# Seven block products for eight in the second MLP matrix of a transformer block, with sums of the squares on GpSimd

## The chip, the cores and the metric

The kernel runs on one core of a Trainium2 chip. The metric is the device time of one execution in microseconds (us); lower is better. All matrices are 32-bit floats; matmuls run in the replicated form `float32r`, and every factor is split into a high and a low part (H and L), so that one product of two 128-row tiles is three matmuls: H by H, H by L, L by H.

## The reference

One layer of a diffusion block on a latent stream of 1024 tokens by 1024 channels: a mixer (attention and a state-space branch), then a squared-ReLU MLP. The change touches only the MLP and what is done with its result:

```python
def sq_relu_mlp(h, w1, b1, w2, b2):
    return jnp.square(jax.nn.relu(h @ w1 + b1)) @ w2 + b2

h2_l = modulate(rms_norm(x, norm2_g[l]), sh2_l, sc2_l)
x = x + g2_l * sq_relu_mlp(h2_l, w_mlp1[l], b_mlp1[l], w_mlp2[l], b_mlp2[l])
```

Here `h` is 1024 x 1024, `w1` is 1024 x 4096, `w2` is 4096 x 1024. The squares between the two matrices are called s below, transposed: 4096 rows (hidden units) by 1024 columns (tokens).

## The kernel before

The MLP is the last part of the kernel. All loads and stores are issued from SyncE's one queue, in order. Each engine takes its own instructions in order; for the MLP that order comes out of a planner that places each instruction at the time at which its cost model finds it ready, except for the first 14 loads of the first matrix, where TensorE's order is that of the text.

**First matrix (`first`, `mlp1`).** It already takes seven products of 2 x 2 blocks for eight (the Winograd form of Strassen). The hidden units are taken in 16 pairs of 128-row tiles; the tokens are two halves of 512. For each pair two 512 KB weight tiles r1 and r2 come into `wr` (three buffers). VectorE forms sums of them (`cs`, one buffer; `c4`, one buffer; in place in r2), and `wsplit` makes the H part on ScalarE and the L part on GpSimd (`wH`, `wL`, four buffers). The products B11 and B21 of 14 pairs are made ahead by `first`; the loop over `mlp1(p)` then makes T2, T1, T3, B22 and T4, each 12 matmuls into one PSUM bank (`mm`, six buffers). VectorE adds the products up (`u2`, `u4`, `u3`), and `c_out` adds the bias, ScalarE applies ReLU and square, and the 128 x 512 block of squares is stored to a DRAM tensor `s_d`.

**Second matrix.** No blocks are saved. The 32 tiles of s (128 hidden units by 1024 tokens) and of w2 (128 by 1024) are loaded, split (both L parts on GpSimd), and taken in batches of one, one, thirteen times two, and four tiles. For each batch all 8 x 2 blocks of the output are multiplied into PSUM (three matmuls a tile) and added by VectorE to an accumulator `acc` in SBUF. In the last batch VectorE also multiplies by the gate row `g2row` and adds the residual, and the rows are stored. `mod2` is a small vector product that makes the gate row; ten steps of it run among the batches.

The pools of the first matrix (`h2a`, `n2`, `ml`, `h2b`) are left before the pool `mq` of the second is opened over the same space. The first two tiles of the second matrix are prepared ahead in the pool `wp`, which lives on.

Of the kernel before, what the change touches and what calls it, by code (L numbers as in the profile page):

```python
# [48 lines left out]
def block_kernel(ctx, tc, io, out, dbg=None):  # L49
    nc = tc.nc  # L50
    V, S, G, T = nc.vector, nc.scalar, nc.gpsimd, nc.tensor
    LD = nc.sync
# [47 lines left out]
    wp = ctx.enter_context(pool("wp"))  # L100
    dr = ctx.enter_context(pool("dr", space=DRAM))
# [17 lines left out]
    def wload(src, shape):  # L119
        raw = wp.tile([128, 1024], F32, name="wr", tag="wr", bufs=3)  # L120
        LD.dma_start(raw[:, :int(np.prod(shape))].rearrange("p (a b) -> p a b", a=shape[0]), src)
        return raw

    def wtile(src, shape, scale_row=None, low=None, raw=None):

        n = int(np.prod(shape))
        if raw is None:
            raw = wload(src, shape)
        H = wp.tile([128, 1024], F32R, name="wH", tag="wH", bufs=4)
        L = wp.tile([128, 1024], F32R, name="wL", tag="wL", bufs=4)  # L130
        if scale_row is not None:
            sr = scale_row if shape[0] == 1 else scale_row[:, None, :].to_broadcast([128, shape[0], shape[1]])
            rr = raw[:, :n] if shape[0] == 1 else raw[:, :n].rearrange("p (a b) -> p a b", a=shape[0])
            V.tensor_tensor(rr, rr, sr, op=OP.mult)
        S.activation(H[:, :n], raw[:, :n], AF.Copy)  # L135
        (low or G).tensor_tensor(L[:, :n], raw[:, :n], H[:, :n], op=OP.subtract)  # L136
        return H, L

    def mm3(ps, pairs):

        n = len(pairs)
        for i, (lH, lL, rH, rL) in enumerate(pairs):
# [229 lines left out]
    ws_u, acc = [], []  # L372
# [32 lines left out]
    todo = [(q, kk) for q in range(1, 4) for kk in range(4)]  # L405
# [12 lines left out]
    for q in range(4):  # L418
# [5 lines left out]
        if q == 0:  # L424
# [6 lines left out]
            p = trb()  # L431
            for i in range(3):
# [12 lines left out]
                            op=OP.mult)  # L445
# [173 lines left out]
    for nm in ("re", "im"):  # L619
        p = trb()  # L620
# [122 lines left out]
    for g8 in range(0, NG, 16):  # L743
        p = trb()
# [608 lines left out]
    def mmc():  # L1353
        return psC.tile([128, 512], F32, name="mm", tag="mm", bufs=6)
# [271 lines left out]
    NP = 16  # L1626
    NA = 14
    t1_d = dr.tile([NA, 128, 512], F32, name="t1_d")
    s_d = dr.tile([32, 128, 1024], F32, name="s_d")

    def w1_raw(ft):
        return wload(w1[:, ft * 128:(ft + 1) * 128].rearrange("(a p) n -> p a n", p=128), (8, 128))
# [13 lines left out]
    def r_tile():
        return ml.tile([128, 512], F32, name="r", tag="r", bufs=3)

    def act_out(r, ft, f):
        S.activation(r, r, AF.Square)  # L1650
        LD.dma_start(s_d[ft][:, f * 512:(f + 1) * 512], r)

    def b1(ft):
        return cols[:, R_B1 + ft:R_B1 + ft + 1]

    def c_out(ps, add, ft, f):
        r = r_tile()
# [23 lines left out]
    def mlp1(p):  # L1681
        r1, r2 = w1_raw(2 * p), w1_raw(2 * p + 1)
        cs = ml.tile([128, 1024], F32, name="cs", tag="cs", bufs=1)
        c4 = ml.tile([128, 512], F32, name="c4", tag="c4", bufs=1)
        a, b = slice(0, 512), slice(512, 1024)
        if p >= NA:
            t1 = first(p, wsplit(r1))
        else:
            t1 = t1_tile()
            LD.dma_start(t1, t1_d[p])  # L1690
        V.tensor_tensor(cs[:, a], r2[:, a], r2[:, b], op=OP.add)
        V.tensor_tensor(cs[:, b], cs[:, a], r1[:, a], op=OP.subtract)
        wc = wsplit(cs)
        V.tensor_tensor(c4, r1[:, b], cs[:, b], op=OP.subtract)
        V.tensor_tensor(r2[:, a], r1[:, a], r2[:, a], op=OP.subtract)
        wr = wsplit(r2)
        w4 = wsplit(c4, 512)
        u2, u3, u4 = (ml.tile([128, 512], F32, name=nm, tag=nm, bufs=1) for nm in ("u2", "u3", "u4"))
        V.tensor_tensor(u2, prod(wc, 1, "T2"), t1, op=OP.add)
        V.tensor_tensor(u4, prod(wc, 0, "T1"), u2, op=OP.add)  # L1700
        p7 = prod(wr, 0, "T3")
        V.tensor_tensor(u3, p7, u2, op=OP.add)
        c_out(p7, u4, 2 * p + 1, 1)
        c_out(prod(w4, 0, "B22"), u4, 2 * p, 1)
        c_out(prod(wr, 1, "T4"), u3, 2 * p + 1, 0)

    man_ = tc.manual_schedule(engines={mybir.EngineType.PE})
    man_.__enter__()
# [9 lines left out]
    def w2_src(ft):
        return w2[ft * 128:(ft + 1) * 128, :].rearrange("p (a n) -> p a n", a=1)

    def s_src(ft):
        return s_d[ft].rearrange("p (a n) -> p a n", a=1)

    pre = [(wtile(s_src(0), (1, 1024)), wtile(w2_src(0), (1, 1024)))]
    ml_.__exit__(None, None, None)
    n2_.__exit__(None, None, None)
    h2a_.__exit__(None, None, None)
    h2b_.__exit__(None, None, None)
    mq = ctx.enter_context(pool("mq", reuse_waits="tile"))
    acc2 = [mq.tile([128, 1024], F32, name=f"acc{t}") for t in range(8)]  # L1730
    bb2 = mq.tile([128, 1024], F32, name="bb2")
    LD.dma_start(bb2, bcast_rows(io["b_mlp2"], 1024))

    def mq_split(raw, nm, bufs):
        H = mq.tile([128, 1024], F32R, name=nm + "H", tag=nm + "H", bufs=bufs)
        L = mq.tile([128, 1024], F32R, name=nm + "L", tag=nm + "L", bufs=bufs)
        S.activation(H, raw, AF.Copy)  # L1737
        G.tensor_tensor(L, raw, H, op=OP.subtract)  # L1738
        return H, L

    def mlp2_tiles(ft):
        rs = wload(s_src(ft), (1, 1024))
        rw_ = mq.tile([128, 1024], F32, name="rw2", tag="rw2", bufs=3)
        LD.dma_start(rw_.rearrange("p (a b) -> p a b", a=1), w2_src(ft))
        return mq_split(rs, "s", 6), mq_split(rw_, "w", 6)

    BL = [[0], [1]] + [[b, b + 1] for b in range(2, 28, 2)] + [[28, 29, 30, 31]]
    NBL = len(BL)
    pre2 = [(mq_split(wload(s_src(1), (1, 1024)), "f", 2), mq_split(wload(w2_src(1), (1, 1024)), "f", 2))]
    m2_todo = list(range(30, 40))  # L1750
    m2a = mq.tile([128, 1024], F32, name="m2a")
    m2r = mq.tile([128, 512], F32, name="m2r")
    for bi, fts in enumerate(BL):
        last_ = bi == NBL - 1
        tiles = (pre, pre2)[bi] if bi < 2 else [mlp2_tiles(ft) for ft in fts]
        for t in range(8):
            if last_:
                xr = mq.tile([128, 1024], F32, name="rw2", tag="rw2", bufs=3)
                LD.dma_start(xr, x2_d[t])
            tk = slice(t * 128, (t + 1) * 128)  # L1760
            for n in range(2):
                o = slice(n * 512, (n + 1) * 512)
                ps = mmc()
                mm3(ps, [(s_[0][:, tk], s_[1][:, tk], w_[0][:, o], w_[1][:, o]) for s_, w_ in tiles])
                a_ = acc2[t][:, o]
                V.tensor_tensor(a_, a_ if bi else bb2[:, o], ps, op=OP.add)  # L1766
                if last_:
                    V.tensor_tensor(a_, a_, g2row[:, o], op=OP.mult)
                    V.tensor_tensor(a_, a_, xr[:, o], op=OP.add)
                    if t == 7:  # L1770
                        LD.dma_start(out_v[t][:, o], a_)
            if last_ and t < 7:
                LD.dma_start(out_v[t], acc2[t])
        if 3 <= bi < 8:
            for _ in range(2):
                mod2(m2_todo.pop(0), m2a, m2r, trc)
            if bi == 7:
# [28 lines left out]
```

## Time and profile before

| | |
|---|---|
| median of 3 runs | 1910.69 us (1907.51 to 1912.46) |
| profiled execution: its time | 1909.88 us |
| profiled execution: its span | 1908.2 us |
| TensorE busy in the span | 1841.1 us (96%) |
| VectorE, ScalarE, GpSimd busy | 1279.1, 691.9, 895.4 us |

The span runs from the first to the last instruction that the profiler saw; the time of the execution is 1.7 us longer. A share of busy time is a mean over stages with different limits, so the stages of the MLP have to be looked at one at a time. PE is TensorE, PEld its weight loads, DVE VectorE, ACT ScalarE, POOL GpSimd, SP SyncE. A matmul's listed duration overlaps with the next one's; what it costs is the distance from one start to the next.

### The profile page before, as it was taken

How to read it: one execution, taken by the hardware profiler on the slowest of the kernel's cores; microseconds unless marked ns; L12 is line 12 of the kernel's file. 1: busy time of each engine (PE TensorE's matmuls, PEld its weight loads, DVE VectorE, ACT ScalarE, POOL GpSimd, SP SyncE). 2: the span in 40 equal slices, each digit the busy share in tenths (PEclk: the TensorE clock that was granted, in tenths of full speed). 3: DMA queues.
4: the chain of work that ended last, by engine and by line, in shares of the span. 5: the costliest groups of instructions: out<-in, count | busy, mean ns of one | idle time of the engine just before them, and what ended most of it. 6: DMA issues, size and time to landing. Idle time of an engine off the chain costs nothing. (4 is left out here: it accounts for less than half of the span.)

```text
span 1908.2 us, 25109 instructions
## 1 busy us (share of the span) xinstructions
PE 1841.1 (96%) x9250; PEld 1402.6 (74%) x9250; DVE 1279.1 (67%) x2194; ACT 691.9 (36%) x1016; POOL 895.4 (47%) x471
## 2 busy tenths in 40 slices
PE   7889999998999999999989999999999999999998
PEld 4668888887776556556547777887888877878887
DVE  5989998738897787777645455486454457545556
ACT  4542222244314555555442121455444541111110
POOL 2232333313425777777784453375444564443330
PEclk9989999999999999999999999999999999999999
DMA  9412222221222000000006664355554465333213
GB/s 308 97 56 71 76 77 78 76 85 46 84 71 78 18 23 23 23 23 18 22 13 207 213 209 144 116 177 182 155 155 152 126 218 178 110 107 104 89 55 144
DMA packets 179339, 200.72 MB, mean 105 GB/s; under 512 B 28112, under 2 KB 128260, under 8 KB 179216
## 3 DMA queue, kind: packets, MB, share of 16 engines
q1 hardware_dynamic: 179216, 199.11, 32.6%
q8 instruction: 73, 1.20, 0.3%
q14 instruction: 50, 0.41, 0.1%
HBM read 154.85 MB, written 44.09 MB: 104 GB/s over the span
## 5 line engine op out<-in xcount | busy, mean ns | idle before, releaser
L1202 POOL TENSOR_TENSOR accP<-accP,P 128x1024 f32<-128x1024 f32 x96 | 240.9, 2510 | 20.9 <-ACT P L1184 15.7
L1766 DVE TENSOR_TENSOR acc<-acc,mm 128x512 f32<-128x512 f32 x240 | 162.5, 686 | 127.6 <-PE mm L145 127.6
L136 POOL TENSOR_TENSOR wL<-wr,wH 128x1024 fp32r<-128x1024 f32 (+1 forms) x58 | 135.9, 2351 | 197.9 <-ACT wH L135 187.0
L1184 ACT ACTIVATE P<-sT 128x1024 f32<-128x1024 f32 x160 | 163.8, 1026 | 116.6 <-PE sT L1180 114.1
L1088 DVE TENSOR_REDUCE m<-mx 128x1 f32<-128x512 f32 x240 | 154.5, 686 | 76.1 <-PE mx L1086 69.7
L143 PE MATMUL mm<-wH,sH 128*128 128x512 f32 x480 | 187.3, 390 | 1.3 <-DVE acc L1766 1.2
L144 PE MATMUL mm<-wL,sH 128*128 128x512 f32 x480 | 186.8, 389 | 0.0
L145 PE MATMUL mm<-wH,sL 128*128 128x512 f32 x480 | 186.7, 389 | 0.0
L1197 PE MATMUL pv<-P,Vt 128*64 128x512 f32 x640 | 150.5, 600 | 0.0
L1738 POOL TENSOR_TENSOR sL<-wr,sH 128x1024 fp32r<-128x1024 f32 x30 | 72.2, 2406 | 152.0 <-ACT sH L1737 152.0
L135 ACT ACTIVATE wH<-wr 128x1024 fp32r<-128x1024 f32 (+1 forms) x62 | 61.9, 1005 | 216.2 <-PE mm L144 96.4
L1737 ACT ACTIVATE sH<-wr 128x1024 fp32r<-128x1024 f32 x30 | 31.6, 1054 | 226.5 <-issue 160.7
L1177 PE MATMUL sT<-Q,KH 128*128 128x512 f32 x320 | 105.3, 410 | 2.2 <-ACT P L1184 2.2
L143 PEld LDWEIGHTS mm<-wH,sH 128*128 128x128 f32 x480 | 90.1, 188 | 22.5 <-DVE acc L1766 2.9
L145 PEld LDWEIGHTS mm<-wH,sL 128*128 128x128 f32 x480 | 90.1, 188 | 18.9
L144 PEld LDWEIGHTS mm<-wL,sH 128*128 128x128 f32 x480 | 90.1, 188 | 18.2
L143 PE MATMUL mm<-hH,wH 128*128 128x512 f32 x248 | 101.1, 408 | 0.0
L1180 PE MATMUL sT<-Q,K 65*128 65x512 f32 x320 | 100.9, 396 | 0.0
L145 PE MATMUL mm<-hH,wL 128*128 128x512 f32 x248 | 97.7, 394 | 0.0
L144 PE MATMUL mm<-hL,wH 128*128 128x512 f32 x248 | 97.3, 392 | 0.0
L1197 PEld LDWEIGHTS pv<-P,Vt 128*64 128x64 f32 x640 | 41.7, 136 | 71.6 <-issue 62.3
L1666 POOL TENSOR_TENSOR wL<-wr,wH 128x1024 fp32r<-128x1024 f32 x32 | 76.8, 2405 | 36.6 <-ACT wH L1665 36.6
(581 smaller groups left out, 4722.8 us busy)
## 6 DMA issues: line engine op xcount, KB each, us to landing
wr<-in_w_mlp_dram SPq DMA_DIRECT2D x48, 512.0 KB
wr<-in_w_in_dram SPq DMA_DIRECT2D x35, 512.0 KB
wr<-in_w_mod_dram SPq DMA_DIRECT2D x32, 512.0 KB
s_d<-r SPq DMA_DIRECT2D x64, 256.0 KB
wr<-s_d SPq DMA_DIRECT2D x32, 512.0 KB
rw<-in_w_mlp_dram SPq DMA_DIRECT2D x30, 512.0 KB
x<-in_x_dram SPq DMA_DIRECT2D x12, 512.0 KB
xt<-in_w_mod_dram SPq DMA_DIRECT2D x24, 256.0 KB
```

What stands on the lines that cost most here:

```text
L136: (low or G).tensor_tensor(L[:, :n], raw[:, :n], H[:, :n], op=OP.subtract)
L143: T.matmul(ps, lH, rH, start=i == 0, stop=False)
L144: T.matmul(ps, lH, rL, start=False, stop=False)
L145: T.matmul(ps, lL, rH, start=False, stop=i == n - 1)
L1088: V.tensor_reduce(m3[:, 4 * j + t, c:c + 1], m, axis=AX.X, op=OP.max)
L1177: T.matmul(o, KH[kv][:, ks], Q1[:, j], start=True, stop=False)
L1180: T.matmul(o, K2[kv][:, ks], Q2[:, j], start=False, stop=True)
L1184: S.activation(P, sT, AF.Exp, scale=HD ** -0.5)
L1197: T.matmul(pv[64 * j:64 * j + 64, :], Vt[:, kt, kv * 64:kv * 64 + 64], P[:, j * 512:(j + 1) * 512], start=kt == 0, stop=kt == NK - 1)
L1202: G.tensor_tensor(accP, accP, P, op=OP.add)
L1666: (low or G).tensor_tensor(L[:, :n], raw[:, :n], H[:, :n], op=OP.subtract)
L1766: V.tensor_tensor(a_, a_ if bi else bb2[:, o], ps, op=OP.add)
```

## The change

In the first matrix: the low part of `cs` is made on VectorE instead of GpSimd. The three blocks of squares that `mlp1` makes go to the buffers `xs4` (free since the norm), the fourth, made earlier by `first`, is read back from DRAM into the same buffers; GpSimd forms the four sums S3, S1, S2, S4 of blocks, and SyncE stores them. So for each pair six 128 x 512 blocks are stored after `first` where there were three, and one more is loaded.

In the second matrix: the output's 2 x 2 blocks (512 tokens by 512 channels) are made from seven products. Each product runs over all 8 blocks of hidden units (`NB`), that is 8 steps of 24 matmuls, and its four PSUM banks are held over all 8 steps; VectorE or ScalarE empties them once, at the end of the product. One factor of a step is a stored block of squares or sum of them, the other a quadrant of w2 or a sum, which VectorE forms in place in SBUF (`Q1`, `Q12`, `Q22`). A step's L parts are made on GpSimd and VectorE, for one step in three on VectorE alone. The gate and the residual are applied to each output block when it is done, in the middle of later products.

```diff
-    s_d = dr.tile([32, 128, 1024], F32, name="s_d")
+    NB = NP // 2
+    sc_d = dr.tile([NB, 7, 128, 1024], F32, name="sc_d")
+    SC = ("A11", "A12", "A22", "S1", "S2", "S3", "S4")
...
     def act_out(r, ft, f):
         S.activation(r, r, AF.Square)
-        LD.dma_start(s_d[ft][:, f * 512:(f + 1) * 512], r)
+        if (ft % 2, f) != (0, 1):
+            LD.dma_start(sc_at(ft // 2, ("A11", "A12", "A22")[ft % 2 + f]), r)
...
-        wc = wsplit(cs)
+        wc = wsplit(cs, low=V)
...
-        c_out(p7, u4, 2 * p + 1, 1)
-        c_out(prod(w4, 0, "B22"), u4, 2 * p, 1)
-        c_out(prod(wr, 1, "T4"), u3, 2 * p + 1, 0)
+        k = 2 * (p % 2)
+        a11, a12, a21, a22 = xs4[k][:, a], xs4[k][:, b], xs4[k + 1][:, a], xs4[k + 1][:, b]
+        LD.dma_start(a11, sc_at(p, "A11"))
+        c_out(p7, u4, 2 * p + 1, 1, a22)
+        c_out(prod(w4, 0, "B22"), u4, 2 * p, 1, a21)
+        c_out(prod(wr, 1, "T4"), u3, 2 * p + 1, 0, a12)
+        for nm, x, y, op in (("S3", a11, a21, OP.subtract), ("S1", a21, a22, OP.add), ("S2", None, a11, OP.subtract),
+                             ("S4", a12, None, OP.subtract)):
+            t = hf_tile()
+            G.tensor_tensor(t, sl if x is None else x, sl if y is None else y, op=op)
+            LD.dma_start(sc_at(p, nm), t)
+            sl = t
...
+    PR = [("A11", "B11"), ("S1", "T1"), ("A12", "B21"), ("S3", "T3"), ("S2", "T2"), ("A22", "T4"), ("S4", "B22")]
+    todo = [(j, b) for j in range(7) for b in range(NB)]
...
+    OPS = {b: (wtile(sc_src(b, "A11"), (1, 1024)), wtile(w2_q(b, "B11"), (2, 512))) for b in range(2)}
...
+    def rs_load(src, n=1024):
+        r = mq.tile([128, 1024], F32, name="rs", tag="rs", bufs=4)[:, :n]
+        LD.dma_start(r.rearrange("p (a n) -> p a n", n=src.shape[-1]), src)
+        return r
...
+    def operands(n):
...
+        for raw, E in ((RW.pop(n), V if n % 3 == 2 else G), (t, V)):
+            p, tg, bufs = (mq, "f", 2) if n % 3 == 2 else (wp, "w", 4)
+            H = p.tile([128, 1024], F32R, name=tg + "H", tag=tg + "H", bufs=bufs)
+            L = p.tile([128, 1024], F32R, name=tg + "L", tag=tg + "L", bufs=bufs)
+            S.activation(H, raw, AF.Copy)
+            E.tensor_tensor(L, raw, H, op=OP.subtract)
...
+        if b == 0:
+            pss = [mmc() for _ in range(4)]
+        (sH, sL), (tH, tL) = OPS.pop(n)
+        for i in range(4):
+            for h in range(2):
+                tk, o = slice(512 * h + 128 * i, 512 * h + 128 * i + 128), slice(512 * h, 512 * h + 512)
+                T.matmul(pss[i], sH[:, tk], tH[:, o], start=b == 0 and h == 0, stop=False)
+                T.matmul(pss[i], sH[:, tk], tL[:, o], start=False, stop=False)
+                T.matmul(pss[i], sL[:, tk], tH[:, o], start=False, stop=b == NB - 1 and h == 1)
+            if b == NB - 1:
+                evac(j, i, pss[i])
```

## Rows read from the trace of the kernel before

**Rows 1.** The page: busy time, share of the span, instructions of each engine.

```profile
PE 1841.1 (96%) x9250; PEld 1402.6 (74%) x9250; DVE 1279.1 (67%) x2194; ACT 691.9 (36%) x1016; POOL 895.4 (47%) x471
```

**Rows 2.** Windows: stretch, its us, busy by engine, clock, DMA share, GB/s.

```profile
1312.60:1502.00 189.40, 187.90 (x829) 155.34 (x828) 96.23 (x139) 86.44 (x128) 84.51 (x43) 1.00 0.51 157
...
1545.10:1560.00 14.90, 10.74 (x35) 8.27 (x34) 8.21 (x13) 8.94 (x10) 13.56 (x6) 0.77 0.82 304
1560.00:1903.20 343.20, 341.92 (x1499) 280.04 (x1497) 200.11 (x282) 53.95 (x56) 135.73 (x57) 1.00 0.35 117
```

**Rows 3.** Timeline of TensorE, one pair of the first matrix: start, duration.

```profile
1409.80 0.39 PE L1641 MATMUL mm<-T2H,wH 128*128 128x512 f32 x1
1412.52 0.39 PE L1641 MATMUL mm<-T1H,wH 128*128 128x512 f32 x1
...
1423.40 0.39 PE L1641 MATMUL mm<-T2H,wH 128*128 128x512 f32 x1
```

**Rows 4.** Timeline of VectorE, the same pair, and `c` seven pairs later.

```profile
1402.78 0.69 DVE L1694 TENSOR_TENSOR c<-wr,cs 128x512 f32<-128x512 f32 x1 [2.60 <-POOL wL L1666]
...
1408.32 1.12 DVE L1691 TENSOR_TENSOR cs<-wr 128x512 f32<-128x512 f32 x1 [4.18 <-DMA wr<-in_w_mlp_dram]
1409.36 0.68 DVE L1699 TENSOR_TENSOR u<-mm,t 128x512 f32<-128x512 f32 x1
...
1412.36 1.39 DVE L1658 SCALAR_TENSOR_TENSOR r<-mm,cols,u 128x512 f32<-128x512 f32 x2
...
1497.77 0.69 DVE L1694 TENSOR_TENSOR c<-wr,cs 128x512 f32<-128x512 f32 x1 [2.60 <-POOL wL L1666]
```

**Rows 5.** Timeline of GpSimd, the same pair.

```profile
1406.49 2.40 POOL L1666 TENSOR_TENSOR wL<-wr,wH 128x1024 fp32r<-128x1024 f32 x1 [0.51 <-ACT wH L1665]
1415.02 1.30 POOL L1666 TENSOR_TENSOR wL<-c,wH 128x512 fp32r<-128x512 f32 x1 [6.13 <-ACT wH L1665]
```

**Rows 6.** Timelines of ScalarE and SyncE, the same pair.

```profile
1414.33 0.61 ACT L1665 ACTIVATE wH<-c 128x512 fp32r<-128x512 f32 x1
...
1403.50 0.38 SPq L121 DMA_DIRECT2D wr<-in_w_mlp_dram  x1
```

**Rows 7.** Timelines of GpSimd and VectorE where both work on SBUF.

```profile
1254.08 1.74 POOL L1570 TENSOR_TENSOR B22L<-hf,B22H 128x512 fp32r<-128x512 f32 x1
...
1252.99 1.67 DVE L1574 TENSOR_TENSOR hf<-hf,B11L 128x512 f32<-128x512 f32 x1
```

**Rows 8.** Groups of instructions, second matrix and others: count, busy us, mean ns.

```profile
L143 PE MATMUL mm<-wH,sH 128*128 128x512 f32 x480 | 187.3, 390 | 1.3 <-DVE acc L1766 1.2
L1766 DVE TENSOR_TENSOR acc<-acc,mm 128x512 f32<-128x512 f32 x240 | 162.5, 686 | 127.6 <-PE mm L145 127.6
L136 DVE TENSOR_TENSOR wL<-wr,wH 128x1024 fp32r<-128x1024 f32 x4 | 4.8, 1212 | 0.0
L1738 POOL TENSOR_TENSOR sL<-wr,sH 128x1024 fp32r<-128x1024 f32 x30 | 72.2, 2406 | 152.0 <-ACT sH L1737 152.0
L1737 ACT ACTIVATE sH<-wr 128x1024 fp32r<-128x1024 f32 x30 | 31.6, 1054 | 226.5 <-issue 160.7 <-PE mm L144 50.8 <-DMA wr<-s_d 14.7
```

**Rows 9.** Timelines of SyncE, VectorE and TensorE at the change of matrices.

```profile
1540.54 5.22 SPq L1651 DMA_DIRECT2D s_d<-r  x3
1545.86 0.38 SPq L1732 DMA_DIRECT2D bb<-in_b_mlp_dram  x1
...
1550.73 5.68 DVE L1766 TENSOR_TENSOR acc<-bb,mm 128x512 f32<-128x512 f32 x9 [6.65 <-DMA bb<-in_b_mlp_dram]
...
1551.48 0.79 PE L143 MATMUL mm<-wH 128*128 128x512 f32 x1 [4.16 <-DVE acc L1766]
```

**Rows 10.** The chain that ended last, its end.

```profile
1903.21 0.70 DVE acc L1766
1903.93 0.70 DVE acc L1768
1904.65 0.69 DVE acc L1769
```

More of the change, by code (lines that the diff above doesn't have):

```diff
@@ L1628, in block_kernel, with sc_at @@
     t1_d = dr.tile([NA, 128, 512], F32, name="t1_d")
-    s_d = dr.tile([32, 128, 1024], F32, name="s_d")
+    NB = NP // 2
+    sc_d = dr.tile([NB, 7, 128, 1024], F32, name="sc_d")
+    SC = ("A11", "A12", "A22", "S1", "S2", "S3", "S4")
+    def sc_at(p, nm):
+        return sc_d[p // 2, SC.index(nm)][:, (p % 2) * 512:(p % 2) * 512 + 512]
     def w1_raw(ft):
@@ L1650, in act_out, with c_out @@
         S.activation(r, r, AF.Square)
-        LD.dma_start(s_d[ft][:, f * 512:(f + 1) * 512], r)
+        if (ft % 2, f) != (0, 1):
+            LD.dma_start(sc_at(ft // 2, ("A11", "A12", "A22")[ft % 2 + f]), r)
     def b1(ft):
         return cols[:, R_B1 + ft:R_B1 + ft + 1]
-    def c_out(ps, add, ft, f):
-        r = r_tile()
+    def c_out(ps, add, ft, f, r=None):
+        r = r_tile() if r is None else r
         V.scalar_tensor_tensor(r, ps, b1(ft), add, op0=OP.add, op1=OP.add)
@@ L1715, in block_kernel, with one, w2_q, sc_src @@
         mlp1(p)
[L1718 to L1724, printed above, removed]
+    PR = [("A11", "B11"), ("S1", "T1"), ("A12", "B21"), ("S3", "T3"), ("S2", "T2"), ("A22", "T4"), ("S4", "B22")]
+    todo = [(j, b) for j in range(7) for b in range(NB)]
+    def one(src):
+        return src.rearrange("p (a n) -> p a n", a=1)
+    def w2_q(b, nm):
+        e, h = int(nm[1]) - 1, int(nm[2]) - 1
+        return w2[512 * b:512 * b + 512, 512 * h:512 * h + 512].rearrange("(j e p) n -> e p j n", e=2, p=128)[e]
+    def sc_src(b, nm):
+        return one(sc_d[b, SC.index(nm)])
+    OPS = {b: (wtile(sc_src(b, "A11"), (1, 1024)), wtile(w2_q(b, "B11"), (2, 512))) for b in range(2)}
     ml_.__exit__(None, None, None)
@@ L1729, in block_kernel @@
     mq = ctx.enter_context(pool("mq", reuse_waits="tile"))
-    acc2 = [mq.tile([128, 1024], F32, name=f"acc{t}") for t in range(8)]
-    bb2 = mq.tile([128, 1024], F32, name="bb2")
[L1732 to L1750, printed above, removed]
+    RW = {}
@@ new lines, in rs_load @@
+    def rs_load(src, n=1024):
+        r = mq.tile([128, 1024], F32, name="rs", tag="rs", bufs=4)[:, :n]
+        LD.dma_start(r.rearrange("p (a n) -> p a n", n=src.shape[-1]), src)
+        return r
+    for b in range(2, 4):
+        RW[b] = rs_load(sc_src(b, "A11"))
+    Q = {nm: [mq.tile([128, 1024], F32, name=f"{nm}{b}") for b in range(NB)] for nm in ("Q1", "Q12", "Q22")}
+    X1, X2, X3, X5 = ([mq.tile([128, 512], F32, name=f"X{x}{i}") for i in range(4)] for x in (1, 2, 3, 5))
+    bb2 = mq.tile([128, 1024], F32, name="bb2")
@@ L1751, in block_kernel @@
     m2a = mq.tile([128, 1024], F32, name="m2a")
     m2r = mq.tile([128, 512], F32, name="m2r")
[L1753 to L1777, printed above, removed]
-                LD.dma_start(g2row, bcast_rows(m2_d[3], 1024))
@@ new lines, in q_load, with loads @@
+    def q_load(nm, b, src):
+        LD.dma_start(Q[nm][b].rearrange("p (a n) -> p a n", a=2), w2_q(b, src))
+    def loads(n):
+        j, b = todo[n]
+        if n not in RW and n > 1:
+            RW[n] = rs_load(sc_src(b, PR[j][0]))
+        if j in (0, 1, 3):
+            q_load(*{0: ("Q1", b, "B11"), 1: ("Q12", b, "B12"), 3: ("Q22", b, "B22")}[j])
+        elif j in (2, 5):
+            RW[n, 1] = rs_load(w2_q(b, "B21"))
+    def operands(n):
+        if n < 2:
+            return
+        j, b = todo[n]
+        q1, q12, q22 = (Q[nm][b] for nm in ("Q1", "Q12", "Q22"))
+        if j == 1:
+            V.tensor_tensor(q1, q12, q1, op=OP.subtract)
+        elif j == 3:
+            V.tensor_tensor(q12, q22, q12, op=OP.subtract)
+        elif j == 4:
+            V.tensor_tensor(q1, q22, q1, op=OP.subtract)
+        elif j == 5:
+            V.tensor_tensor(q1, q1, RW.pop((n, 1)), op=OP.subtract)
+        elif j == 6:
+            qv = q22.rearrange("p (a n) -> p a n", a=2)
+            V.tensor_tensor(qv, qv, g2row[:, None, 512:].to_broadcast([128, 2, 512]), op=OP.mult)
+        t = RW.pop((n, 1)) if j == 2 else q12 if j == 3 else q22 if j == 6 else q1
+        res = []
+        for raw, E in ((RW.pop(n), V if n % 3 == 2 else G), (t, V)):
[4 more added lines that the diff above has]
+            E.tensor_tensor(L, raw, H, op=OP.subtract)
+            res.append((H, L))
+        OPS[n] = res
@@ new lines, in base, with store, evac @@
+    def base(x, t, h):
+        o = slice(512 * h, 512 * h + 512)
+        xr = rs_load(one(x2_d[t][:, o]), 512)
+        V.tensor_tensor(x, x, g2row[:, o], op=OP.mult)
+        V.tensor_tensor(x, x, xr, op=OP.add)
+    def store(x, t, h):
+        LD.dma_start(out_v[t][:, 512 * h:512 * h + 512], x)
+    def evac(j, i, ps):
+        if j == 0:
+            V.tensor_tensor(X1[i], bb2[:, :512], ps, op=OP.add)
+        elif j == 1:
+            V.tensor_tensor(X5[i], bb2[:, 512:], ps, op=OP.add)
+        elif j == 2:
+            V.tensor_tensor(X2[i], X1[i], ps, op=OP.add)
+        elif j == 3:
+            S.activation(X3[i], ps, AF.Copy)
+        elif j == 4:
+            V.tensor_tensor(X1[i], X1[i], ps, op=OP.add)
+        elif j == 5:
+            V.tensor_tensor(X3[i], X3[i], ps, op=OP.subtract)
+        else:
+            V.tensor_tensor(X1[i], X1[i], ps, op=OP.add)
+            store(X1[i], i, 1)
@@ new lines, in block_kernel @@
+    m2_todo = list(range(30, 40))
+    for n in range(3):
+        loads(n)
+    LD.dma_start(bb2, bcast_rows(io["b_mlp2"], 1024))
+    V.tensor_tensor(bb2[:, 512:], bb2[:, 512:], bb2[:, :512], op=OP.subtract)
+    operands(2)
+    for n, (j, b) in enumerate(todo):
+        if n + 3 < len(todo):
+            loads(n + 3)
+        if n + 2 < len(todo) and n:
+            operands(n + 2)
+        if n == 0:
+            operands(1)
+        if b == 0:
[9 more added lines that the diff above has]
+                evac(j, i, pss[i])
+        if 8 <= n <= 26 and n % 2 == 0:
+            mod2(m2_todo.pop(0), m2a, m2r, trc)
+            if not m2_todo:
+                LD.dma_start(g2row, bcast_rows(m2_d[3], 1024))
+        i = b // 2
+        if j == 4 and b % 2 == 0:
+            base(X2[i], i, 0)
+            store(X2[i], i, 0)
+        elif j == 5 and b % 2 == 0:
+            V.tensor_tensor(X3[i], X3[i], X1[i], op=OP.add)
+            V.tensor_tensor(X1[i], X1[i], X5[i], op=OP.add)
+            V.tensor_tensor(X5[i], X5[i], X3[i], op=OP.add)
+            base(X5[i], 4 + i, 1)
+            store(X5[i], 4 + i, 1)
+        elif j == 5:
+            base(X1[i], i, 1)
+        elif j == 6 and b % 2 == 0:
+            base(X3[i], 4 + i, 0)
+            store(X3[i], 4 + i, 0)
```

## Prediction

> **What bounds the kernel now.** I read the page first, then the windows by stage, then the timelines of one pair of the first matrix, the groups of the second, and the change between them. The page has TensorE busy for 96% of the span and VectorE, the next, for 67% [rows 1]. That is a mean, so I looked at the stages. From 1312.6 to 1502 us TensorE is busy for 187.9 of 189.4 us, and from 1560.0 to 1903.2 us for 341.9 of 343.2 us, at full granted clock [rows 2]. So in both matrices the path that sets the end is TensorE's own matmuls, and the groups say the same: VectorE waited 127.6 us in 162.5 us of work for products to end, while matmuls waited 1.3 us [rows 8].
>
> What one matmul costs is the distance from start to start. A pair of the first matrix has five products of 12 matmuls, and T2 starts at 1409.80 and again at 1423.40 us [rows 3]: 13.60 us for 60 matmuls, 0.2267 us each. The second matrix has 32 tiles x 16 blocks x 3 = 1536 of them, 348.2 us. It lasts from the end of the first, near 1543.1, to 1903.2 us, 360.1 us. Of the difference, 6.5 us lie in one place: from 1545.1 to 1560.0 us there are 35 matmul records; 37 at the pace of before would take 8.4 of these 14.9 us [rows 2]. The granted clock is 0.77 there, so the stall cost more than its 4.16 us of waiting [rows 9].
>
> The first matrix has a second thing running almost as slowly as TensorE. VectorE's `c` starts at 1402.78 and, seven pairs later, at 1497.77 us [rows 4]: 13.57 us a pair, against TensorE's 13.60. None of the waits in that ring names TensorE: `c` waits for GpSimd's low part of the last `c` [rows 4]; its end frees the weight buffer, and SyncE issues the next load at 1403.50 [rows 6]; `cs` waits for that load until 1408.32 and, behind it in VectorE's queue, come the sums `u` and the two `c_out` at 1412.36 [rows 4]; ScalarE's ReLU and square follow, then its high part of `c` at 1414.33 [rows 6], then GpSimd's low part at 1415.02 [rows 5]. The ring has 0.03 us a pair to spare. There is one reserve besides: `u2` at 1409.36 frees its PSUM bank by 1410.04 us [rows 4], and T1 takes the bank at 1412.52 [rows 3], 2.5 us later.
>
> **Matmuls removed.** The new second matrix has 7 products x 8 steps x 24 = 1344 matmuls of the same shape: 192 fewer, 192 x 0.2267 = 43.5 us. Nothing on TensorE is added. This is the only large term, and it counts in full if every step's operands come within 24 x 0.2267 = 5.44 us.
>
> **The tail.** After the last matmul VectorE now does an addition, a gate product and a residual sum, 0.70 + 0.70 + 0.69 us [rows 10], then the store. Afterwards the last block needs one addition; the gate is already in the factor. That saves 1.4 us.
>
> **The change of matrices.** The stall of before came from the bias row: its load stands behind the last store of squares in SyncE's queue, was issued at 1545.86, and VectorE's first addition, and with it the PSUM banks, waited until 1550.73 [rows 9]. The first emptying of PSUM is now 8 steps later, so this wait goes (at most 6.5 us). But the loads into the new pool again stand behind the last store, which is now that of S4: a square, then a sum on GpSimd, some 2 us later. The steps prepared ahead last 2 x 5.44 = 10.9 us where they lasted 21.8, and the third step's two tiles are the first and the fifth of five 512 KB loads. At the 304 GB/s of that stretch [rows 2] these 2.6 MB take 8.6 us from about 1548, so to 1556.6, then 1.05 us for a high part and 1.21 for a low part on VectorE [rows 8]: 1558.9, against 1556.0 when TensorE wants it. So 2.9 us of a new stall with some loss of clock. Bounds: a gain of 6.5 us and a loss of 4; I take a gain of 3.2.
>
> **The sums in the first matrix.** For each pair GpSimd loses a low part of 1024 columns, 2.40 us, and gains four sums of 512, each like its low part of `c`, 1.30 us [rows 5]: 2.40 + 1.30 + 4 x 1.30 = 8.9 us of work in 13.6, where it had 6.1. VectorE gains the low part of `cs`, 1.21 us [rows 8]; with four sums of 0.68, three `u` of 0.68 and three `c_out` of 0.70 it has 8.1 us. Neither is too much as a sum. But they slow each other: where both work on SBUF alone, GpSimd's 512 columns take 1.74 instead of 1.30 us and VectorE's 1.67 instead of 0.68 [rows 7]. So each waits for the other's instruction: 1.74 is about 1.30 plus what VectorE's needs. In the ring, `c` and `cs` are such instructions; `c` now meets sums that are ready when GpSimd has finished the low part of `c`, and `cs` meets GpSimd's low part of `wr` until 1408.89 already [rows 4, 5]. Also six stores instead of three and one load more take the traffic of a pair from 2.1 to 3.1 MB, 231 GB/s; at 157 GB/s the DMA engines were 51% busy [rows 2], so 75%, and the 4.8 us of the load in the ring may grow. Bounds: nothing, if the sums fall into GpSimd's idle 6.1 us [rows 5]; or a whole sum in front of both, 2.6 us a pair, over 13 pairs 13 x (2.6 - 0.03) - 2.5 = 31 us. Half a sum in front of each, an instruction found in progress, gives 1.3 us a pair and 13 x 1.27 - 2.5 = 14 us. I take that.
>
> The longer queue on SyncE is in the same estimate: a store of a sum waits for GpSimd, and behind it stand the next pair's weight loads. The reads of A11 are issued a whole product before GpSimd needs them, and cost nothing while that holds.
>
> **Supply of the new second matrix.** Per step ScalarE has two high parts, 2.1 us; GpSimd 2/3 of a low part, 1.6 us; VectorE 1.33 low parts and 0.71 operand sums of 1.21 us, with outputs and `mod2` 199 us in all, 3.6 us a step, against 5.44. With every GpSimd operation in its way (36 x 2.41 = 87 us) VectorE would have 286 us for 305. In the sixth product, with three output sums and the gate of two blocks for every two steps, VectorE and GpSimd together have about 6.8 us a step, so it runs on the reserve of operands made ahead. The DMA moves 63 MB in 305 us, 207 GB/s; at 117 GB/s the share was 0.35 [rows 2], so about 0.62. At the six product boundaries two of the four banks are free at once, the others after one addition of 0.69 us [rows 8] each. I charge one such addition a boundary, 4 us; the bounds are nothing, and the cost of the last rival below.
>
> **Sum.** 1909.9 (the profiled execution: span 1908.2 and 1.7 around it, 0.8 us under the median) - 43.5 - 1.4 - 3.2 + 14 + 4 = 1879.8 us; I say 1880.
>
> **The rivals.**
> *Everything is hidden.* The sums fall into GpSimd's gap and the boundaries cost nothing: 1909.9 - 43.5 - 1.4 - 3.2 = 1861.8, down to 1858.5 if the change of matrices is smooth too. For it: all engines but TensorE have room as sums. Against it: the ring's 0.03 us.
> *The first matrix is bound by the ring in full*, 31 us, with the second at its 4: 1909.9 - 43.5 - 1.4 - 3.2 + 35 = 1896.8; with no gain at the change of matrices and a clock lost there, 1904. For it: two instructions of the ring need what GpSimd's sums hold. The Trainium skill ("SBUF — State Buffer", "SBUF: two separate sides") says that an operation of VectorE with two SBUF inputs and one of GpSimd take the shared ports as a lock for the whole instruction, and that the other is blocked until then. By that rule every meeting costs the rest of the other's instruction, and the whole-sum price is this rival; the rows on both engines agree with a wait and not with a shared speed [rows 7].
> *The second matrix is bound by its operands: slower.* One step's chain in engine order is an operand sum 1.21, two high parts 2.1, VectorE's low part 1.21, and 2.4 if GpSimd's low part is in front: 6.9 us. If the planner's order lets one step's chain begin only where the last one's ended, as the ring of the first matrix shows that it can, 54 steps take 54 x (6.9 - 5.44) = 79 us too long: 1880 - 4 + 79 = 1955. It decides from about 6.1 us a step, where it eats the 34 us that are left. Against it: three sets of operand buffers.
>
> **How the numbers follow.** Chances: the forecast (1868 to 1891) 0.44, all hidden (1857 to 1867) 0.18, the ring in full (1892 to 1904) 0.18, an even end (1905 to 1916) 0.06, slower 0.14. The range from 1857 to 1904 holds the first three, 0.80. A measurement of this kernel tells about 0.3%, 6 us, from no change: faster 0.80, same 0.06, slower 0.14.
>
> **What would show it.** The second matrix from its first to its last matmul near 310 us, with 1344 starts 0.2267 us apart and waits of TensorE only at the first step from the new pool and at product boundaries. In the first matrix, T2 starts about 14.9 us apart instead of 13.60, and TensorE waiting for VectorE (a bank) or GpSimd (a low part of `c`). If T2 stays at 13.60, the 14 us are wrong. If TensorE waits for low parts within products of the second matrix, the last rival holds. A low granted clock anywhere but at the change would make it wrong as well.

## The result, and the profile after

The changed kernel takes 1921.67 us (median of 5 runs, 1918.51 to 1926.43) against 1911.87 us before (5 runs): a ratio of 1.0054, 95% interval 1.0032 to 1.0075. It is slower by half a per cent. The forecast was 1880 us in a range from 1857 to 1904; the time lies above it.

The page has the span at 1920.0 us, TensorE busy for less, all others for more than in [rows 1]:

```profile
PE 1814.2 (94%) x9058; PEld 1367.3 (71%) x9058; DVE 1359.4 (71%) x2103; ACT 743.0 (39%) x1068; POOL 949.7 (49%) x495
```

The 192 matmuls are gone (9058 for 9250). From the starts and ends of matmuls by stage, the 11.8 us between the two spans divide as follows (us; "lost" is what a stretch took beyond its matmuls at 0.2267 us):

| | before | after | difference | forecast |
|---|---|---|---|---|
| up to the first matrix | 1231.9 | 1232.7 | +0.8 | 0 |
| first matrix | 311.2 | 340.6 | +29.4 | +14 |
| lost at the change of matrices | 6.5 | 15.3 | +8.8 | -3.2 |
| second matrix, its matmuls | 348.2 | 304.7 | -43.5 | -43.5 |
| second matrix, lost otherwise | 5.4 | 23.0 | +17.6 | +4 |
| after the last matmul | 5.0 | 3.7 | -1.3 | -1.4 |
| sum | 1908.2 | 1920.0 | +11.8 | -30.1 |

TensorE's timeline in the changed kernel answers to [rows 3, 9]; the bracket is how long it stood idle, and for whom:

```profile
1434.72 0.39 PE L1648 MATMUL mm<-T2H,wH 128*128 128x512 f32 x1
...
1444.96 0.50 PE L1649 MATMUL mm<-B22H,wL 128*128 128x512 f32 x1 [0.85 <-POOL wL L1674]
...
1450.31 0.39 PE L1648 MATMUL mm<-T2H,wH 128*128 128x512 f32 x1
...
1584.85 0.79 PE L1861 MATMUL mm<-wL,wH 128*128 128x512 f32 x1 [5.69 <-POOL wL L136]
...
1598.46 1.22 PE L1860 MATMUL mm<-fH 128*128 128x512 f32 x2 [6.05 <-ACT fH L1809]
...
1686.04 0.79 PE L1862 MATMUL mm<-wH,wL 128*128 128x512 f32 x1 [7.39 <-POOL wL L1810]
...
1826.61 0.50 PE L1860 MATMUL mm<-wH 128*128 128x512 f32 x1 [2.47 <-DVE X L1834]
```

T2 now comes 15.59 us apart instead of 13.60, and from the third pair on TensorE waits in nearly every pair for GpSimd's low part of `c`. There are two waits at the change of matrices and one of 7.39 us in the second. Of the 23.0 us lost otherwise in the second matrix 10.5 lie in the third of its seven products, around that wait, and 8.0 in the sixth and seventh, where TensorE waits for VectorE: 2.47 us for a PSUM bank (the last line), then 2.02 and 1.45 us for low parts.

**The first matrix.** VectorE's, GpSimd's and SyncE's timelines of the same pair, to be read against [rows 4, 5, 6]:

```profile
1436.96 2.28 DVE L1700 TENSOR_TENSOR cs<-cs,wr 128x512 f32<-128x512 f32 x1
...
1444.94 1.76 DVE L1702 TENSOR_TENSOR c<-wr,cs 128x512 f32<-128x512 f32 x1 [2.58 <-POOL wL L1674]
```

```profile
1435.85 2.84 POOL L1674 TENSOR_TENSOR wL<-wr,wH 128x1024 fp32r<-128x1024 f32 x1
1443.63 1.27 POOL L1674 TENSOR_TENSOR wL<-c,wH 128x512 fp32r<-128x512 f32 x1 [4.93 <-ACT wH L1673]
1444.86 1.29 POOL L1720 TENSOR_TENSOR hf<-xs,xs 128x512 f32<-128x512 f32 x1
```

```profile
1446.72 0.38 SPq L121 DMA_DIRECT2D wr<-in_w_mlp_dram  x1
```

`c` still waits for GpSimd's low part of the last `c`. When that ends, GpSimd starts a sum at 1444.86, before VectorE's `c` at 1444.94, and `c` takes 1.76 instead of 0.69 us. The second half of `cs` meets the low part of `wr`, which four sums have pushed later, and takes 2.28 instead of 0.68. Together 2.67 us; the first half of `cs` and the load give a little back, and the ring stands at 15.57 us. SyncE issues the next weight load at 1446.72, just as `c` ends (1446.70), so no store stood in its way here.

**The second matrix.** Here is where the 7.39 us come from. The first fence is GpSimd, the second VectorE:

```profile
1667.36 18.62 POOL L1810 TENSOR_TENSOR wL<-rs,wH 128x1024 fp32r<-128x1024 f32 x1 [0.57 <-ACT wH L1809]
```

```profile
1672.34 2.34 DVE L1795 TENSOR_TENSOR Q<-Q,Q 128x1024 f32<-128x1024 f32 x2
1674.62 2.34 DVE L1797 TENSOR_TENSOR Q<-Q,Q 128x1024 f32<-128x1024 f32 x2
1676.89 1.21 DVE L1810 TENSOR_TENSOR wL<-rs,wH 128x1024 fp32r<-128x1024 f32 x1
...
1681.43 2.34 DVE L1810 TENSOR_TENSOR fL<-rs,fH 128x1024 fp32r<-128x1024 f32 x2
1683.70 2.46 DVE L1828 TENSOR_TENSOR X<-bb,mm 128x512 f32<-128x512 f32 x4
```

One low part of GpSimd lasts 18.62 us, where [rows 8] have 2.41. From 1667.80 VectorE works back to back on SBUF alone, 14 instructions at 1.14 us from start to start. At 1683.70 VectorE turns to PSUM, and 2.3 us later GpSimd is done. What VectorE is busy with is not urgent: L1795 and L1797 are the operand sums of the fourth and fifth products, run while TensorE is at the end of the second.

### The profile page after: what moved, and what is told of

It reads as the page before. It is cut to its first block, busy times and chain, and to the rows that moved or that the text cites. A ratio compares the mean times of both kernels' runs of the same rounds, so it can differ in the third digit from the quotient of the medians.

```text
span 1920.0 us, 24749 instructions
## 1 busy us (share of the span) xinstructions
PE 1814.2 (94%) x9058; PEld 1367.3 (71%) x9058; DVE 1359.4 (71%) x2103; ACT 743.0 (39%) x1068; POOL 949.7 (49%) x495
## 5 line engine op out<-in xcount | busy, mean ns | idle before, releaser
L136 POOL TENSOR_TENSOR wL<-wr,wH 128x1024 fp32r<-128x1024 f32 (+1 forms) x60 | 142.8, 2391 | 185.7 <-ACT wH L135 174.2
L1810 POOL TENSOR_TENSOR wL<-rs,wH 128x1024 fp32r<-128x1024 f32 x36 | 128.0, 3558 | 189.5 <-ACT wH L1809 180.1
L1861 PE MATMUL mm<-wL,wH 128*128 128x512 f32 x304 | 120.9, 398 | 9.6 <-POOL wL L136 5.7
L1862 PE MATMUL mm<-wH,wL 128*128 128x512 f32 x304 | 120.5, 396 | 7.7 <-POOL wL L1810 7.7
L1860 PE MATMUL mm<-wH 128*128 128x512 f32 x304 | 120.5, 396 | 2.5 <-DVE X L1834 2.5
L212 PE MATMUL mm<-wL,hH 128*128 128x512 f32 (+1 forms) x216 | 83.5, 387 | 8.9 <-POOL wL L136 8.8
L1809 ACT ACTIVATE wH<-rs 128x1024 fp32r<-128x1024 f32 x41 | 43.0, 1059 | 125.7 <-issue 80.4
L1177 PEld LDWEIGHTS sT<-Q,KH 128*128 128x128 f32 x320 | 55.1, 188 | 50.4 <-issue 26.0
L210 PE MATMUL mm<-wH,hH 128*128 128x512 f32 (+1 forms) x216 | 82.8, 386 | 4.7 <-DVE qn L983 2.9
L1667 ACT ACTIVATE xs<-xs 128x512 f32<-128x512 f32 x48 | 30.0, 625 | 139.5 <-DVE xs L1666 139.5
```

The costliest lines, as they stand in the source:

```text
L1177: T.matmul(o, KH[kv][:, ks], Q1[:, j], start=True, stop=False)
L1810: E.tensor_tensor(L, raw, H, op=OP.subtract)
L1860: T.matmul(pss[i], sH[:, tk], tH[:, o], start=b == 0 and h == 0, stop=False)
L1861: T.matmul(pss[i], sH[:, tk], tL[:, o], start=False, stop=False)
L1862: T.matmul(pss[i], sL[:, tk], tH[:, o], start=False, stop=b == NB - 1 and h == 1)
```

## The experiments

Where no count is given, a time is that of a single run; the kernel before, timed beside each, took 1910.7 to 1911.6 us.

**The sums on GpSimd left out.** The four blocks are stored as they are in place of the sums; all stores and loads remain, though these stores no longer wait for GpSimd.

```diff
-            t = hf_tile()
-            G.tensor_tensor(t, sl if x is None else x, sl if y is None else y, op=op)
-            LD.dma_start(sc_at(p, nm), t)
-            sl = t
+            LD.dma_start(sc_at(p, nm), {"S3": a21, "S1": a22, "S2": a11, "S4": a12}[nm])
```

> GpSimd's four sums of squares are left out; the blocks themselves are stored in their place, so every store, load and wait on SyncE stays (the output is not the reference's). Theory A (the sums on GpSimd lengthen the ring of VectorE, ScalarE, GpSimd and the weight load): the distance of T2 starts falls from 15.57 to about 13.6 us, the first matrix ends near 1546 instead of 1573 us, and the kernel takes about 1895 us. Rival B (the six stores and the read-back, on SyncE's queue and on the DMA, lengthen the load in the ring): T2 stays at 15 us or more and the kernel near 1920 us.

It took 1888.49 us, and the second matrix began at 1548.1 instead of 1573.3 us. From the fifth pair on TensorE's timeline has T2 13.6 us apart, and VectorE's has both instructions at their old length:

```profile
1428.45 0.39 PE L1648 MATMUL mm<-T2H,wH 128*128 128x512 f32 x1
...
1442.06 0.39 PE L1648 MATMUL mm<-T2H,wH 128*128 128x512 f32 x1
```

```profile
1416.52 0.68 DVE L1700 TENSOR_TENSOR cs<-cs,wr 128x512 f32<-128x512 f32 x1
...
1422.91 0.69 DVE L1702 TENSOR_TENSOR c<-wr,cs 128x512 f32<-128x512 f32 x1 [2.60 <-POOL wL L1674]
```

So GpSimd's sums are what lengthens the ring; in these pairs the six stores, the read-back and VectorE's low part of `cs` cost TensorE nothing. Rival B falls. The pairs before them were not free: the first matrix takes 317.6 us in this run, against 311.2 before the change. In one of them SyncE and VectorE show

```profile
1337.65 4.13 SPq L1719 DMA_DIRECT2D sc_d<-xs  x3
1341.84 0.43 SPq L121 DMA_DIRECT2D wr<-in_w_mlp_dram  x1
```

```profile
1346.81 0.69 DVE L1699 TENSOR_TENSOR cs<-wr 128x512 f32<-128x512 f32 x1 [7.67 <-DMA wr<-in_w_mlp_dram]
```

Here a weight load did stand behind stores, and that interval of T2 was 16.72 us. The second matrix is shorter as well, 334.8 us for 343.0: without the sums the wait of 5.69 us at its start is gone.

**A second buffer for `c`.**

```diff
-        return ml.tile([128, 512], F32, name="r", tag="r", bufs=3)
+        return ml.tile([128, 512], F32, name="r", tag="r", bufs=2)
...
-        c4 = ml.tile([128, 512], F32, name="c4", tag="c4", bufs=1)
+        c4 = ml.tile([128, 512], F32, name="c4", tag="c4", bufs=2)
```

> c4 gets two buffers (one of three r buffers is given up), sums and traffic as in the changed kernel. Theory A (a ring, not a lack of throughput): c no longer waits for GpSimd's low part of the last c, the weight load is issued about 8 us earlier, T2 comes every 13.6 us, the first matrix ends near 1546 us and the kernel takes about 1895 us. Rival C (VectorE and GpSimd together have too much work on SBUF, 12 of 13.6 us, for any order): T2 stays at 15 us or more, about 1918 us.

1921.83 us: T2 every 15.30 us, hardly better. The wait of `c` for the old buffer is gone, but VectorE's instructions, now in a row, wait for GpSimd one after the other:

```profile
1445.88 1.67 DVE L1699 TENSOR_TENSOR cs<-wr 128x512 f32<-128x512 f32 x1
1447.47 0.68 DVE L1707 TENSOR_TENSOR u<-mm,t 128x512 f32<-128x512 f32 x1
1448.08 1.18 DVE L1700 TENSOR_TENSOR cs<-cs,wr 128x512 f32<-128x512 f32 x1
1449.18 1.78 DVE L1703 TENSOR_TENSOR wr<-wr 128x512 f32<-128x512 f32 x1
1450.88 2.88 DVE L1702 TENSOR_TENSOR c<-wr,cs 128x512 f32<-128x512 f32 x1
```

Four instructions of 0.68 us take 7.51; the one between them that reads PSUM (`mm`) takes its 0.68. The numbers are rival C's, and this run alone does not tell too much work from meetings in a ring. My theory of a ring that one buffer opens missed: the new ring runs through VectorE and ScalarE alone, and the 4.8 us of waits in it are the same meetings with GpSimd.

**The sums on VectorE.** With the second buffer for `c`, and the low part of `cs` back on GpSimd:

```diff
-        wc = wsplit(cs, low=V)
+        wc = wsplit(cs)
...
-            G.tensor_tensor(t, sl if x is None else x, sl if y is None else y, op=op)
+            V.tensor_tensor(t, sl if x is None else x, sl if y is None else y, op=op)
```

> First matrix only: the four sums of squares go to VectorE, the low part of cs back to GpSimd, c4 has two buffers. Theory A2 (in the ring VectorE's instructions wait for those of GpSimd; with the sums on VectorE they cost 4 x 0.6 us and block nothing): T2 comes every 13.6 to 14.2 us, the first matrix ends near 1548 us and the kernel takes about 1898 us. Rival C2 (VectorE's own work, now about 10 us a pair, in one ring with ScalarE is the limit): T2 every 15 us or more, 1915 us or more.

1900.08 us, 21.6 less than the changed kernel; the second matrix begins at 1557.3. T2 comes every 14.84 us, between the two theories' numbers; the total is near theory A2's. The second matrix, which this edit does not touch, gave 5.6 of the 21.6 us (337.4 for 343.0), at its start.

**VectorE in the order of the text**, in the second matrix.

```diff
+    man_ = tc.manual_schedule(engines={mybir.EngineType.DVE})
+    man_.__enter__()
     for n in range(3):
         loads(n)
...
             store(X3[i], 4 + i, 0)
+    man_.__exit__(None, None, None)
```

> VectorE's instructions in the second matrix keep the order of the text instead of the planner's. Theory D (the planner runs eight steps' operand sums back to back on VectorE, and GpSimd's one low part stands 18.6 us behind them, so TensorE waits 7.4 us): no GpSimd low part takes over 6 us, the 7.4 us wait is gone, the second matrix falls from 342 to about 330 us and the kernel takes about 1909 us. Rival E (VectorE lacks time in the second matrix): the waits come back elsewhere, 1918 us or more, or VectorE waits in order for ScalarE and it is slower.

1923.19 us. The wait of 7.39 us is gone, as theory D says, but the second matrix still lasts 340.3 us, of which nearly 16 are lost at the change, as before. In the sixth product TensorE waits about 1.2 us in each of several steps for high and low parts, and in the seventh once 5.13 us. I put this down to the order: the text puts each step's sum, high part and low part right behind one another, and VectorE waits in order for ScalarE. That is rival E's second half, but 1923 us is within the changed kernel's own spread, and the run does not separate lack of time from order.

**All low parts of the second matrix on VectorE** (those of the loop's steps, in the planner's order again).

```diff
-        for raw, E in ((RW.pop(n), V if n % 3 == 2 else G), (t, V)):
+        for raw, E in ((RW.pop(n), V), (t, V)):
```

> Second matrix only: all low parts on VectorE, GpSimd idle there. Theory D (GpSimd's low part is locked out while VectorE works back to back): the wait of 7.4 us goes, no wait for a low part over 3 us is left within products, the second matrix falls from 342 to about 332 us, 1911 us. Rival E (VectorE lacks time): 36 more low parts of 1.14 us are 41 us more on VectorE, 4.2 us a step and 5.5 in the sixth product; TensorE waits there for low parts, 1920 us or more.

1903.23 us; the second matrix takes 323.2 instead of 343.0. Windows of the same stretch, first of the changed kernel, then of this one (columns as in [rows 2]):

```profile
1611.50:1891.50 280.00, 265.90 (x1147) 215.39 (x1146) 211.60 (x170) 100.07 (x102) 117.79 (x32) 0.98 0.51 180
```

```profile
1611.50:1891.50 280.00, 280.00 (x1231) 229.92 (x1230) 208.12 (x210) 104.24 (x106) 0.00 (x0) 1.00 0.55 184
```

TensorE is busy throughout, and every product but the first and the fourth takes what its matmuls cost. VectorE runs 210 instructions instead of 170 and is busy for 208 us instead of 212. That stretch holds more steps of this kernel than of the changed one; over the whole second matrix the work of both is the same, and the windows are, again first of the changed kernel:

```profile
1573.30:1920.00 346.70, 317.11 (x1349) 255.92 (x1347) 237.67 (x191) 114.66 (x117) 137.75 (x42) 0.97 0.53 188
```

```profile
1574.60:1901.50 326.90, 312.49 (x1350) 254.97 (x1348) 225.82 (x227) 114.81 (x117) 9.84 (x6) 0.98 0.58 199
```

With 36 low parts more, VectorE is busy for 225.8 us instead of 237.7: the low parts that it took over cost it less than the waits that it got rid of. Theory D holds with double the gain, since GpSimd's low parts had also held up VectorE; rival E (VectorE lacks time) falls. The planner's order, with operand sums far ahead, does no harm when nobody is locked out by it.

**The change of matrices.** First the block that comes back from DRAM, in the last two pairs.

```diff
-            t1 = first(p, wsplit(r1))
+            t1 = first(p, wsplit(r1), xs4[2 * (p % 2)][:, 0:512])
...
-        LD.dma_start(a11, sc_at(p, "A11"))
+        if p < NA:
+            LD.dma_start(a11, sc_at(p, "A11"))
```

> In the last two pairs the block A11 goes straight from c_out to its buffer instead of through DRAM. Theory F (at the change of matrices GpSimd stands at its sum for a block that comes back from DRAM, and the low part of the second step stands behind it): GpSimd's wait of 2.9 us goes, TensorE's waits of 5.7 and 6.0 us at the change shrink to about 3 and 4, 1915 us. Rival G (the loads into the new pool behind the last store decide): the two waits stay, 1920 us.

1925.82 us. The first wait shrinks from 5.69 to 1.93 us, the second grows from 6.05 to 7.65: theory F holds for the first, rival G for the second, and the kernel is no faster. GpSimd's and SyncE's timelines of the changed kernel show what stands in front: on GpSimd a sum that waits for the block from DRAM, then the low part that TensorE waits for; on SyncE, before the loads, the stores of the last sums, blocked for 4.83 us.

```profile
1577.33 1.29 POOL L1720 TENSOR_TENSOR hf<-xs,xs 128x512 f32<-128x512 f32 x1 [2.89 <-DMA xs<-sc_d]
...
1581.48 3.32 POOL L136 TENSOR_TENSOR wL<-wr,wH 128x1024 fp32r<-128x1024 f32 x1
1584.76 1.27 POOL L1720 TENSOR_TENSOR hf<-xs,hf 128x512 f32<-128x512 f32 x1
```

```profile
1581.54 4.83 SPq L1721 DMA_DIRECT2D sc_d<-hf  x2
...
1586.94 0.89 SPq L1762 DMA_DIRECT2D rs<-sc_d  x2
1587.92 1.89 SPq L1775 DMA_DIRECT2D Q<-in_w_mlp_dram  x3
```

Then the third step's raw tiles were loaded ahead into the old `wr` buffers, three early loads of w2 put later, and one low part of the second step made on VectorE.

```diff
-    OPS = {b: (wtile(sc_src(b, "A11"), (1, 1024)), wtile(w2_q(b, "B11"), (2, 512))) for b in range(2)}
+    OPS = {b: (wtile(sc_src(b, "A11"), (1, 1024)), wtile(w2_q(b, "B11"), (2, 512), low=V if b else G)) for b in range(2)}
+    raw2 = [wload(sc_src(2, "A11"), (1, 1024)), wload(w2_q(2, "B11"), (2, 512))]
...
-    for b in range(2, 4):
-        RW[b] = rs_load(sc_src(b, "A11"))
+    RW[2], RW[2, 1] = raw2
+    RW[3] = rs_load(sc_src(3, "A11"))
...
+        if 2 <= n < 5:
+            q_load("Q1", n - 2, "B11")
```

> Change of matrices only: the raw tiles of the third step are loaded ahead into the old wr buffers, three early loads of w2 that are wanted only eight steps later come later, and one low part of the second step is on VectorE. Theory G (the third step waits for loads that stand behind the last store and share the DMA with others): the waits of 5.7 and 6.0 us fall to under 2 us each, the loss there from 16 to about 4 us, 1909 us. Rival: the fourth step waits in place of the third, 1917 us or more.

1905.33 us. Waits of 4.89 and 1.45 us are left, now at the fourth step, so theory G and its rival are both partly right. The second matrix takes 327.4 us, 15.6 less. Of this 6.8 us were won in the first product, where the change lies, and 8.3 in the third: the wait of 7.39 us is all but gone there (0.3 us) in the planner's new order, and so is not owed to the loads.

**All three together.**

> All three edits together. If the three causes are separate and add up (24 us in the first matrix, 10 within the second, 12 at the change): about 1875 us, faster than both. If VectorE, which now has the sums and all low parts, becomes the bound: 1895 us or more.

1872.61 us (4 runs), 0.9793 of the kernel before (0.9776 to 0.9809). The three edits alone had saved 21.6, 18.4 and 16.3 us; together they save 49. The time is near the 1875 us of causes that add up, and VectorE does not become the bound. What is left is the first matrix, where T2 still comes every 14.84 us. VectorE's timeline shows why, with GpSimd's below:

```profile
1457.60 2.25 DVE L1720 TENSOR_TENSOR hf<-hf,xs 128x512 f32<-128x512 f32 x1
1459.77 0.68 DVE L1699 TENSOR_TENSOR cs<-wr 128x512 f32<-128x512 f32 x1
1460.37 2.87 DVE L1720 TENSOR_TENSOR hf<-xs,hf 128x512 f32<-128x512 f32 x1
```

```profile
1456.72 2.57 POOL L1674 TENSOR_TENSOR wL<-cs,wH 128x1024 fp32r<-128x1024 f32 x1 [0.86 <-ACT wH L1673]
1460.04 2.65 POOL L1674 TENSOR_TENSOR wL<-wr,wH 128x1024 fp32r<-128x1024 f32 x1 [0.75 <-ACT wH L1673]
```

Two sums stand until GpSimd's low parts end. Three kernels move these low parts of the first matrix's loop to VectorE, by `low=V` in `wsplit`: all of them, that of `cs`, that of `c`.

> As g1_all, and the low parts of the loop of the first matrix are all on VectorE, so GpSimd has nothing there and no instruction can wait for another engine's. Theory A3 (what is left of the ring, 14.84 us a pair, is two sums on VectorE of 2.25 and 2.87 us that wait for GpSimd's low parts): T2 comes every 13.6 us and the kernel takes about 1857 us. Rival C3 (VectorE's 11.5 us a pair in order, with ScalarE's turns between, are a ring of 14 us or more themselves): 1870 us or more.

> As g1_all, with the low part of cs on VectorE as in the changed kernel, that of wr and c on GpSimd. Theory A3: only one low part of 2.4 us is left in VectorE's way; T2 every 13.6 to 14.2 us, about 1862 us. Rival C3: as g1_all or slower, 1872 us.

> As g1_all, with the low part of c on VectorE, those of cs and wr on GpSimd. It takes GpSimd out of the chain from c to product B22, where TensorE waits 0.86 us a pair, but leaves both low parts of 2.4 us in the way of VectorE's sums. Theory A3 (those two waits make the ring): T2 stays near 14.8 us, 1871 us. Rival (the low part of c is what TensorE waits for): 13.6 us, 1857 us.

| low parts on VectorE | us, 4 runs each | ratio to before, interval | second matrix begins at |
|---|---|---|---|
| all | 1857.40 | 0.9727 (0.9708 to 0.9745) | 1542.3 |
| `cs` | 1860.15 | 0.9738 (0.9722 to 0.9753) | 1546.9 |
| `c` | 1873.15 | 0.9797 (0.9777 to 0.9816) | 1553.5 |

The first matrix takes 313.7, 317.0 and 324.8 us in them, against 325.9 with the three edits alone; the third kernel's earlier begin of the second matrix lies mostly in the stages before. Theory A3 is borne out by all three. Taking GpSimd out of the step that TensorE was seen to wait for (`c`) left T2 at 14.85 us; taking its long low parts out of VectorE's way gave the time back. With all on VectorE the two matrices are as TensorE's matmuls make them:

```profile
1310.00:1500.00 190.00, 187.49 (x821) 154.78 (x820) 162.79 (x233) 86.56 (x128) 2.56 (x1) 0.99 0.68 227
1542.30:1850.40 308.10, 307.38 (x1349) 252.01 (x1347) 229.08 (x231) 115.52 (x117) 1.05 (x1) 1.00 0.60 208
```

The kernel with all of them on VectorE is faster than both the kernel before and the changed one.

## Why the prediction was wrong

Between the forecast of 1879.8 us and 1921.67 us lie 41.9. Three terms of the sum carry 41.0 of them: the sums in the first matrix (29.4 us for 14), the change of matrices (a loss of 8.8 for a gain of 3.2) and the supply of the second (17.6 for 4). In the first two the mechanism was named and the price too low; in the third the mechanism was missing from the sum.

*Bound, matmuls, tail.* Right. The stages were TensorE's, 192 matmuls at 0.2267 us went, and the tail saved 1.3 us for 1.4. The best kernel's 1857.4 us, reached with further edits, is at the low end of the range and below the rival "everything is hidden" (1861.8): the saving was there to be had.

*"Half a sum in front of each, an instruction found in progress, gives 1.3 us a pair."* The mechanism was right, the size wrong. From the fourth pair on the ring grew by 2.0 us a pair. Of its two meetings `c` met a whole sum (1.07 us), because GpSimd's next sum starts as its low part ends and VectorE, which waits for that very end, comes 0.08 us later. The other was with the low part of `wr`, which I had counted as it stood before; the sums had pushed it onto the second half of `cs`, 1.60 us. I had also stopped at pair 13, and the last two pairs lost time too: T2 came 22.24 and 24.82 us apart where it was 19.04, 9.0 us of the 29.4. There GpSimd's low part of `c` stood behind three sums in GpSimd's own queue, and TensorE waited 2.03 us for it. So it is in part luck that 29.4 us lie near the 31 of the whole-sum bound. The charge that I let DMA and SyncE share in was hardly theirs: without the sums and with all the traffic T2 came every 13.6 us from the fifth pair on, after a loss of 6.4 us in the pairs before.

*"A gain of 3.2" at the change.* The mechanism was named and the bound was too low: 2.9 us of stall were forecast. By the prediction's own terms it should have been 4.9, since 1543.1 + 10.9 is 1554.0 us and not 1556.0. I had counted the loads behind the last store, but not that this store's sum stood on GpSimd behind a block on its way through DRAM, nor that the last low part of the second step stood in that queue too, behind three sums and before the fourth. Two waits of 5.69 and 6.05 us, with a granted clock of 0.83 in the 40 us around them, lost 15.3 us.

*"With every GpSimd operation in its way VectorE would have 286 us for 305."* This is the step that failed: the second matrix lost 17.6 us more than before, where 4 were forecast. I priced VectorE waiting for GpSimd and called the sum of the work safe; I did not price GpSimd waiting for VectorE, which has no bound in its own work. The rival of operands that come too late was right in sign and in place, and wrong in its chain: not sum, high part and low part in a row, but one low part shut out for 18.62 us, while VectorE made operand sums for later products. With no low part left on GpSimd those losses went. The trace of before did show single meetings [rows 7], and no long ones (2406 ns on average for 30 low parts), which fits, since VectorE's work in the second matrix read PSUM [rows 8] and did not meet GpSimd's.

*The chances.* Slower had 0.14, and each of three mis-sized terms had its cases. But the first and the third hung on one thing, VectorE and GpSimd in SBUF at once, so they went wrong together, and I had added them as if they were apart. The change had mostly causes of its own, the order on GpSimd and on SyncE's queue.

## What to carry to other kernels

Work moved to an idle GpSimd is not free if VectorE works from SBUF at the same time: as a bound, count for each of VectorE's instructions on the path that read two tiles of SBUF a whole GpSimd instruction, and for each GpSimd instruction the whole stretch of such VectorE work that may run without a gap. In the second matrix VectorE did the work sooner alone than with help: moving 36 low parts to it made it less busy, not more. And where a ring of waits is within 0.2% of the bound, any edit to it is an edit to the critical path, and the buffers named in it are only one of its links.

## What was not expected of the hardware

One 128x1024 subtraction on GpSimd lasted 18.62 us while VectorE ran two-input instructions on SBUF 1.14 us apart, and ended 2.3 us after VectorE turned to PSUM. In [rows 7] the two had taken turns, one for one, at 1.7 us each; there each of VectorE's sums needs the one before it, and in the long case they are independent. That alone does not decide it. Some 16 us before, in the same stage, GpSimd got in after one instruction, although VectorE's next (L1797, into `Q1`) does not need the one in front of it (L1795, into `Q12`):

```profile
1650.85 1.21 DVE L1795 TENSOR_TENSOR Q<-Q,Q 128x1024 f32<-128x1024 f32 x1
1651.99 3.42 DVE L1797 TENSOR_TENSOR Q<-Q,Q 128x1024 f32<-128x1024 f32 x1
```

```profile
1651.04 3.28 POOL L1810 TENSOR_TENSOR wL<-rs,wH 128x1024 fp32r<-128x1024 f32 x1 [2.33 <-ACT wH L1809]
```

What decides between one instruction and fourteen stays open. The Trainium skill ("SBUF — State Buffer", "SBUF: two separate sides") has the loser blocked for the other's whole instruction. The trace agrees for single meetings: those of 1.76, 2.28 and 2.87 us each end 0.55 us after GpSimd's instruction. It shows besides that the block can run on, here over 14 instructions that follow without a gap.
